# RMSNorm and matmul on one core: two stores cut at row 60, and the last two tiles stored whole

## The chip, the cores and the metric

One core of one Trainium2 chip. The time is the device time of one execution in microseconds (us); several executions are taken in turn with the kernel before on the same chip. The span in a profile is 1.8 us shorter than the time (210.6 against 212.46). A run counts as slow when it is over 1.5% above the fastest of the same kernel. Ratios use fast runs alone; medians are of all runs unless said.

## The reference

```python
x: (16, 1024, 512) float32, gamma: (512,), weight: (512, 768)
rms = np.sqrt(np.mean(x ** 2, axis=-1, keepdims=True) + eps)
x_norm = x / rms * gamma
return np.matmul(x_norm, weight).astype(np.float32)
```

The rows of x are 16384. They make 128 tiles of 128 rows. The kernel reads 33.6 MB of x and writes 50.3 MB.

## The kernel before

Tiles go in groups of 8 (16 groups). A group has one buffer of x and one of the output. It is loaded and stored in pieces given by `parts`; a piece of n tiles has n rows of DRAM in each of its 128 partitions, so a partition's run is n x 3072 B in a store (the trace has 24576 B in a store of 8 tiles, 6144 B in one of 2). Loads and stores are issued by SyncE in program order. GpSimd casts x to bf16, TensorE transposes it two pairs of tiles ahead of the matmuls, VectorE copies the transposes back, ScalarE takes the norms, and ScalarE and VectorE scale the output in turn.

```python
parts = {0: [1, 2, 1, 2, 2], 1: [4, 4], NG - 2: [4, 2, 2], NG - 1: [2, 2, 1, 1, 1, 1]}
...
def store(i):
    if i == first[i] + size[i] - 1:
        nc.sync.dma_start(out=rows(out, i), in_=held(o_tiles, first[i], size[i]))
...
for j in range(2, NP):
    load_until(2 * j + AHEAD)
    if j == NP // 2:
        marks = singles.tile([8, 2, 256], F32)
        for c, n in enumerate((5, 6)):
            nc.sync.dma_start(out=marks[:n, c, :128 + 8 * c], in_=x[:n, :128 + 8 * c])
    ...
for i in (NT - 2, NT - 1):
    for lo, hi, engine, queue in ((0, WIDE, nc.scalar, nc.scalar), (WIDE, O, nc.vector, nc.sync)):
        ...
        queue.dma_start(out=rows(out, i)[:, 0, lo:hi], in_=dst)
```

`marks` is never read. Its two loads have 5 and 6 rows of odd sizes, which makes their packets easy to find in a trace.

## Time and profile before

| | before |
|---|---|
| time, median of 3 runs (lowest to highest) | 212.46 us (212.32 to 212.94) |
| span, TensorE busy, SyncE's DMA queue busy | 210.6 us, 95%, 96.4% |
| last arithmetic ends, last store lands | 204.1 us, 209.8 us |

Two more views are needed for the comparison. First the chain of waits, by engine:

```profile
## 4 chain that ended last, share of the span: by engine, by line
PE 90%; DMA 3%; DVE 1%; ACT 1%; issue 1%; SPq 0%; DVEq 0%
```

TensorE holds nearly all of the chain. Then who waits for whom (total us, times, longest us):

```profile
POOL xb L86 <- PE tp L113: 69.4, 39, 2.0
POOL xb L86 <- DMA xt<-in_x_dram: 50.2, 16, 6.0
```

GpSimd waits more often for TensorE to free a buffer (39 times) than for a load (16 times). TensorE's only wait for a cast of GpSimd is 0.2 us: loads come in time.

The most useful records are in no summary view: the single DMA packets, with start, duration and size, and the 16 landings of a DMA on its semaphore, one from each DMA engine. A packet starts 3 to 4 ns before the one ahead of it on the same engine ends, so the packets can be strung into 16 chains, one for each DMA engine. Below, "chain" means that.

### The profile page before, as it was taken

The page shows a single profiled execution, that of the slowest core. Times are in us where ns is not written, and L with a number is a line of the kernel's source. Part 1 is how long each engine was busy: PE and PEld are TensorE (multiplying, and loading weights), DVE is VectorE, ACT ScalarE, POOL GpSimd, SP SyncE. Part 2 cuts the span into 40 slices and gives each one's busy share as a digit, 9 for nine tenths or more (in the row PEclk, how much of TensorE's full clock was granted, in tenths as well). Part 3 has the DMA queues.
Part 4 walks back from the last instruction along what each step waited for, and adds up shares of the span by engine and source line. Part 5 has one row for each costly group of instructions (what it writes and reads, how often), then busy time and mean ns, then how long its engine had stood idle before and what let it go on. Part 6 is the DMA issues. An engine that isn't in the chain of part 4 may idle for free.

```text
span 210.6 us, 3584 instructions
## 1 busy us (share of the span) xinstructions
PE 200.2 (95%) x1272; PEld 138.0 (66%) x1297; DVE 111.8 (53%) x204; ACT 158.3 (75%) x388; POOL 66.3 (31%) x71
## 2 busy tenths in 40 slices
PE   7999999999999999999999999999999999999960
PEld 2466766766776676677667666776667677766630
DVE  1555655654565456446645654565456446645630
ACT  4489777787778778877877787778778877887830
POOL 1057433423333233323242332334233323140000
PEclk9999999999999999999999999999999999999997
DMA  6999999999999999999999999999999999999892
GB/s 202 401 427 426 392 436 408 418 437 437 431 425 425 414 446 418 432 434 417 429 429 437 416 440 439 417 439 414 440 408 443 393 438 369 439 406 412 358 382 98
DMA packets 8956, 85.70 MB, mean 407 GB/s; under 512 B 1245, under 2 KB 1514, under 8 KB 5098
## 3 DMA queue, kind: packets, MB, share of 16 engines
q1 hardware_dynamic: 8374, 84.94, 96.4%
q10 hardware_dynamic: 564, 0.53, 0.7%
q8 instruction: 10, 0.16, 0.3%
q14 instruction: 8, 0.07, 0.1%
HBM read 35.14 MB, written 50.33 MB: 406 GB/s over the span
## 4 chain that ended last, share of the span: by engine, by line
PE 90%; DMA 3%; DVE 1%; ACT 1%; issue 1%; SPq 0%; DVEq 0%
PE ops L147 77%; PE tp L113 13%; DMA w_f<-in_weight_dram 3%; DVE ot L132 1%; ACT ot L130 0%; SPq L75 0%; ACT jk L90 0%; DVE w_bf L132 0%; DVE xT L120 0%; ACT rms L94 0%; DVE rstd L96 0%; DVEq L132 0%
## 5 line engine op out<-in xcount | busy, mean ns | idle before, releaser
L147 PE MATMUL ops<-w_bf,xT 128*128 128x512 bf16 (+1 forms) x999 | 192.5, 324 | 1.5 <-DVE w_bf L132 0.2
L147 PEld LDWEIGHTS <-xT 128*128 128x128 bf16 x1024 | 100.2, 98 | 56.6 <-DVE xT L120 0.9
L86 POOL CAST xb<-xt 128x1024 bf16<-128x1024 f32 (+1 forms) x65 | 65.6, 1016 | 120.2 <-PE tp L113 69.4
L120 DVE COPY xT<-tp 128x1024 bf16<-128x1024 bf16 (+1 forms) x67 | 44.5, 667 | 81.3 <-PE tp L113 81.3
L130 ACT ACTIVATE ot<-ops,rstd 128x768 f32<-128x768 f32 (+1 forms) x65 | 58.1, 894 | 37.6 <-PE ops L147 36.8
L90 ACT ACTIVATE jk<-xt 128x512 bf16<-128x512 f32 x128 | 78.8, 619 | 1.3 <-DMA xt<-in_x_dram 1.3
L113 PE MATMUL tp<-ident_f,xb 128*128 128x128 f32 x256 | 69.2, 275 | 0.4 <-DVE xb L86 0.3
L132 DVE TENSOR_SCALAR ot<-ops,rstd 128x768 f32<-128x768 f32 (+1 forms) x65 | 64.5, 992 | 2.9 <-PE ops L147 2.8
L113 PEld LDWEIGHTS tp<-ident_f,xb 128*128 128x128 f32 x256 | 36.0, 142 | 5.1 <-issue 1.2
L90 ACT ACTIVATION_READ_ACCUMULATOR jk<-xt 128x1 f32 x128 | 24.4, 191 | 0.0
L94 ACT ACTIVATE rms<-ssq,eps_sb 128x2 f32<-128x2 f32 (+1 forms) x64 | 18.9, 295 | 2.0
L96 DVE RECIPROCAL rstd<-rms 128x2 f32<-128x2 f32 (+1 forms) x64 | 9.9, 155 | 3.3 <-ACT rms L94 3.2
L202 PE MATMUL ops<-warm 128*128 128x512 bf16 x15 | 5.7, 531 | 1.2 <-DVE eps_sb L195 1.2
L130 ACT ACTIVATE w_bf<-w_f,g_sb 128x768 bf16<-128x768 f32 x2 | 1.9, 935 | 2.9 <-DMA w_f<-in_weight_dram 2.9
L202 PEld LDWEIGHTS <-warm 128*128 128x128 bf16 x15 | 1.7, 124 | 3.1 <-issue 1.4
L184 ACT ACT_TABLE_LOAD x1 | 1.3, 1283 | 1.8 <-issue 1.8
L86 DVE CAST xb<-xt 128x512 bf16<-128x512 f32 x2 | 1.2, 594 | 2.5 <-DMA xt<-in_x_dram 2.5
L132 DVE TENSOR_SCALAR w_bf<-w_f,g_sb 128x512 bf16<-128x512 f32 (+2 forms) x3 | 1.4, 485 | 1.3 <-DMA w_f<-in_weight_dram 1.3
L193 DVE MEMSET warm<- 128x256 uint32 x1 | 0.3, 272 | 0.9 <-PEq L308 0.9
L224 PE MATMUL tp<-ident_f,g_row 2*128 2x2 f32 x2 | 0.4, 264 | 0.3 <-DVE xT L120 0.3
L224 PEld LDWEIGHTS tp<-ident_f,g_row 2*128 2x128 f32 x2 | 0.3, 201 | 0.5 <-DVE xT L120 0.5
masks.py:199 POOL TENSOR_SCALAR_AFFINE_SELECT ident_f<-ident_f 128x128 f32<-128x128 f32 x1 | 0.3, 292 | 0.1
(7 smaller groups left out, 0.8 us busy)
## 6 DMA issues: line engine op xcount, KB each, us to landing
out_dram<-ot SPq DMA_DIRECT2D x12, 3072.0 KB, 14.3
xt<-in_x_dram SPq DMA_DIRECT2D x12, 2048.0 KB, 19.1
out_dram<-ot SPq DMA_DIRECT2D x7, 768.0 KB, 9.5
out_dram<-ot SPq DMA_DIRECT2D x3, 1536.0 KB, 11.8
xt<-in_x_dram SPq DMA_DIRECT2D x7, 512.0 KB, 13.8
xt<-in_x_dram SPq DMA_DIRECT2D x3, 1024.0 KB
xt<-in_x_dram SPq DMA_DIRECT2D x6, 256.0 KB, 10.3
w_f<-in_weight_dram SPq DMA_DIRECT2D x2, 768.0 KB, 7.6
```

The source lines that it names most:

```text
L86: engine.tensor_copy(out=xb_tiles[i // 2][:, i % 2:i % 2 + n, :], in_=held(x_tiles, i, n))
L90: nc.scalar.activation(out=jk, in_=held(x_tiles, i)[:, 0, :], func=AF.Square, accum_out=ssq)
L94: nc.scalar.activation(out=rms[:, :n], in_=ssq[:, :n], func=AF.Sqrt, scale=1.0 / D, bias=eps_sb)
L96: nc.vector.reciprocal(out=rstd[:, :n], in_=rms[:, :n])
L113: nc.tensor.transpose(out=tp_tiles[j][:, t, h, :], in_=words[:, lo:lo + P], identity=ident_f)
L120: nc.vector.tensor_copy(out=dst[:, t:t + n, :], in_=src[:, t:t + n, :])
L130: nc.scalar.mul(out=dst, in_=src, mul=r)
L132: nc.vector.tensor_single_scalar(out=dst, in_=src, scalar=r, op=mybir.AluOpType.mult)
L147: nc.tensor.matmul(out=acc[:, lo:hi], lhsT=xT_tiles[i // 2][:, i % 2, k // 2, :, k % 2], rhs=w_bf[:, k, lo:hi], start=(k == 0), stop=(k == ...
L184: nc.scalar.preload_act_table(AF.Sqrt)
L202: nc.tensor.matmul(out=spare[:, :WIDE], lhsT=warm[:, :P], rhs=warm, start=True, stop=True)
L224: nc.tensor.transpose(out=gp[:, c, :], in_=g_row[:, :, c], identity=ident_f[:2, :2])
```

## The change

Its intent: move some bytes from DMA engines that end late to engines that end early, and end the kernel with plain stores. The two-tile stores that end groups 5 and 10 are issued as 60 and 68 rows. The code doesn't say what that does to the engines. After each split 15 chains have 4 rows, four of them 17 more, and one has none. Below, "engines 0 to 3" are those four, "engines 4 to 14" the others of the 15, and "engine 15" the one without; the numbers are names, for no trace here shows an engine's number.

```diff
-    parts = {0: [1, 2, 1, 2, 2], 1: [4, 4], NG - 2: [4, 2, 2], NG - 1: [2, 2, 1, 1, 1, 1]}
+    SPREAD = (NG // 3, 2 * NG // 3)
+    parts = {0: [1, 2, 1, 2, 2], 1: [4, 4], NG - 2: [4, 4], NG - 1: [2, 2, 2, 1, 1]}
+    parts.update({g: [4, 2, 2] for g in SPREAD})
...
-            nc.sync.dma_start(out=rows(out, i), in_=held(o_tiles, first[i], size[i]))
+            dst, src = rows(out, i), held(o_tiles, first[i], size[i])
+            uneven = i // G in SPREAD and i % G == G - 1
+            for lo, hi in ((0, 60), (60, P)) if uneven else ((0, P),):
+                nc.sync.dma_start(out=dst[lo:hi], in_=src[lo:hi])
...
-            if j == NP // 2:
-                marks = ...            # both loads removed
...
-                dst = out_tile(i)[:, lo:hi]
-                scale(engine, dst, a[:, lo:hi], rstd_of[i])
-                queue.dma_start(out=rows(out, i)[:, 0, lo:hi], in_=dst)
+                scale(engine, out_tile(i)[:, lo:hi], a[:, lo:hi], rstd_of[i])
+            store(i)
```

More of the change, by code (lines that the diff above doesn't have):

```diff
@@ L259 @@
             load_until(2 * j + AHEAD)
-            if j == NP // 2:
-                marks = singles.tile([8, 2, 256], F32)
-                for c, n in enumerate((5, 6)):
-                    nc.sync.dma_start(out=marks[:n, c, :128 + 8 * c], in_=x[:n, :128 + 8 * c])
             if j + 3 < NP:
@@ L284 @@
         for i in (NT - 2, NT - 1):
-            for lo, hi, engine, queue in ((0, WIDE, nc.scalar, nc.scalar), (WIDE, O, nc.vector, nc.sync)):
+            for lo, hi, engine in ((0, WIDE, nc.scalar), (WIDE, O, nc.vector)):
                 a = accumulator()
```

## The prediction

> **What bounds the kernel now.** I read the page first, then the chain of waits, the SyncE queue's waits and timeline, the GpSimd timeline, and last the single records of the trace: every DMA packet with start and duration, every landing on a semaphore.
>
> ```profile
> span 210.6 us, 3584 instructions
> ...
> PE 200.2 (95%) x1272; PEld 138.0 (66%) x1297; DVE 111.8 (53%) x204; ACT 158.3 (75%) x388; POOL 66.3 (31%) x71
> ...
> DMA  6999999999999999999999999999999999999892
> GB/s 202 401 427 426 392 436 408 418 437 437 431 425 425 414 446 418 432 434 417 429 429 437 416 440 439 417 439 414 440 408 443 393 438 369 439 406 412 358 382 98
> ...
> q1 hardware_dynamic: 8374, 84.94, 96.4%
> ```
>
> Two resources are full. TensorE is busy 95% of the span, and the chain of waits is TensorE from 9 us to 203.6 us. But the 16 DMA engines are also busy 96% of the time on the one SyncE queue, so each DMA engine always has a backlog. Which of the two sets the end is decided in the last 10 us:
>
> ```profile
> core 0 of [0], span 210.6 us
> start us, us, engine line op out<-in xcount [idle before <-releaser]
> ...
> 202.06 0.33 SPq L144 DMA_DIRECT2D out_dram<-ot  x1
> 202.31 0.48 DVE L132 TENSOR_SCALAR ot<-ops,rstd 128x256 f32<-128x256 f32 x1 [0.28 <-PE ops L147]
> 202.59 0.37 ACTq L291 DMA_DIRECT2D out_dram<-ot  x1
> 203.17 0.69 ACT L130 ACTIVATE ot<-ops,rstd 128x512 f32<-128x512 f32 x1 [0.61 <-PE ops L147]
> 203.61 0.48 DVE L132 TENSOR_SCALAR ot<-ops,rstd 128x256 f32<-128x256 f32 x1 [0.82 <-PE ops L147]
> 203.89 0.35 ACTq L291 DMA_DIRECT2D out_dram<-ot  x1
> 207.61 0.81 SPq L291 DMA_DIRECT2D out_dram<-ot  x2
> ```
>
> ```profile
> engine line waited for: us in total, times, longest us
> ...
> SPq L291 <- DMA out_dram<-ot: 5.2, 1, 5.2
> ```
>
> Compute is over at 204.1 us; SyncE's last two stores go out only at 207.61 us, because the first of them waits 5.2 us for an earlier store: it has the same DMA semaphore as ScalarE's store of 202.59, whose last landing is at 207.55. They land by 209.81, and 0.84 us later the span ends. So the tail is 6.5 us of DMA after the last arithmetic.
>
> Why did that store take 5 us? Its 16 landings are not together: twelve come at 205.39 to 205.52, the others at 205.82, 206.47, 206.62 and 207.55. The store of 199.66 shows the same: twelve by 202.92, four late by 0.6, 1.2, 1.4 and 2.3 us. So a few DMA engines run behind. A packet starts 3 to 4 ns before its predecessor on the same engine ends, so the packets can be strung into 16 chains; the two tiny loads into `marks` (5 rows of 512 B, 6 rows of 544 B) name some of them. Five chains carry both a 512 and a 544 packet, a sixth only a 544. In mid-kernel every chain is gapless. The group-10 store (issued at 145.0) ends on the five marked chains at 155.74, 156.46, 157.07, 157.75 and 159.28, on the others between 155.95 and 160.3. The last of the five is slow by nature: 7.6 us per 3 MB store where the others take 7.27. By the end it is the latest of all.
>
> [...]5 and 6 rows gave 5 and 6 chains, the five contained in the six[...].[...] The trace has 8 KB fetch packets only on four of the five marked chains; their times fit ScalarE (every 54.5 us), VectorE, GpSimd, and, on the slow chain, SyncE.[...] That is an inference.
>
> **The change, part by part.**
>
> 1. *Tail.* Tiles 126 and 127 are stored whole from SyncE. There are eight stores from group 13 on, so the last needs no semaphore still in flight: the 5.2 us wait goes. Tile 126's store can go at about 202.85, tile 127's at 204.15. On a DMA engine that isn't late, the pair store for 124 and 125 (issued 202.06) ends about 205.15, then two times 0.94 us (eight 3072 B rows at 121 ns): 207.0. On today's latest engine: its 199.66 store lands at 205.05, plus four tiles at 0.95: 208.9, plus 0.84 = 209.7. With nothing else changed the span would be 210.65 - 0.9.
>
> 2. *Merged pieces* ([4,4] and [2,2,2,1,1]): the late engines have a backlog anyway, the same bytes follow in order: 0.
>
> 3. *The split stores*, the heart. In groups 5 and 10 the last two tiles (128 rows of 6144 B) go out as 60 rows on 15 engines, 4 each, and 68 rows on 4 engines, 17 each. Before, each engine moved 8 rows. Now engines 0 to 3 move 21 (+13), engines 4 to 14 move 4 (-4), engine 15 none (-8). At 0.23 us a row (234 ns less the overlap) one split is +3.0 us, -0.9 us, -1.85 us; two are +5.9, -1.85, -3.7. The slow engine, if number 4, gains 1.9 us and would finish about 206.8 to 207: good. But engines 0 to 3 never have an idle moment afterwards. They end the group-10 store at 155.74 to 157.75 now. Work left after that on one engine: loads 2 x 2.44 + 3 x 1.26 + 2 x 0.65 = 10.0; stores 3 x 7.27 + 2 x 3.67 + 3 x 1.86 + 2 x 0.95 = 36.6; together 46.6 us. Check with a late chain of today: from 160.29 to its 199.66 store's end my sum gives 43.2, the trace 43.45. The worst of four: 157.07 + 0.7 (part 4) + 5.9 + 46.6 + 0.3 for one more fetch + 0.3 for slow packets = 210.9; VectorE's chain 157.75 + 5.9 + 46.6 + 0.3 = 210.55. Landing 0.3 later, 211.2, plus 0.84: span 212.0, which is 1.4 above 210.65. So two splits overshoot: one would have about levelled the engines.
>
> 4. *Finer loads and SyncE's order.* SyncE issues in program order, and each store in the queue blocks the loads behind it:
>
> ```profile
> 72.12 0.33 SPq L144 DMA_DIRECT2D out_dram<-ot  x1
> 72.54 0.38 SPq L75 DMA_DIRECT2D xt<-in_x_dram  x1
> ```
>
> Now groups 5 and 10 have pieces stored in between, so the load of group 8 waits behind two of them: issued near 81.6 instead of 72.54, and 2.25 MB are queued ahead of it, 5.5 us. The same for group 13 (133.29, then about 142.4). Also groups 5 and 10 load only 1 MB ahead of a store: the queue runs dry for about 0.7 us on early engines (at 48.9; the store's first packet comes about 49.6). Does TensorE feel it? The GpSimd casts:
>
> ```profile
> 153.60 1.04 POOL L86 CAST xb<-xt 128x1024 bf16<-128x1024 f32 x1 [3.07 <-DMA xt<-in_x_dram]
> ...
> 183.36 1.04 POOL L86 CAST xb<-xt 128x1024 bf16<-128x1024 f32 x1 [5.51 <-DMA xt<-in_x_dram]
> ```
>
> The cast of 153.60 waits for group 13's load; its tiles are first transposed at 161.99, so 7.3 us of slack remain. With +5.5 and, on engine 3, +3.0 from its first split, that load lands near 159.9 instead of 153.5: slack about 0.9. The cast of 183.36 has 4.9 us; engines 0 to 3 bring its tiles about 2.5 to 3 us later. So no TensorE stall, narrowly; and one under 3 us would cost nothing, since the DMA ends later.
>
> 5. *Removed marks loads:* 11 packets of 28 ns: nothing.
>
> Sum: -0.9 (tail) and about +2.3 from the new latest engines: span 212.0; the time is 1.8 above the span (212.46 against 210.65): 213.9.
>
> **The rivals.**
> - *The balance works.* If engines 0 to 3 have more room than I give them (other fetches, idle stretches), the end is set by compute and the fast engines: data at 207.4 to 208.5, time 210.1 to 211.2. For it: somebody chose engines 0 to 3 with the marks in view, and four of the five marked chains are early in the trace. Against it: the sum above; their room is only 2 to 4 us, and 5.9 is put there. Weight about 0.35.
> - *The slow engine is one of the four.* It would then carry 6.2 us more on top of 208.4: landing 215, time near 217.6. For it: it is one of five marked, and four of those are loaded.[...] Weight 0.1 to 0.15.
> - *Late loads stall TensorE* more than the narrow slack: adds up to 2 us only where it passes the DMA's end. Small, inside the range.
>
> **Range and chances.** The middle case (half the weight) is 213.9, the first rival pulls the median down: 213.5, range 210.6 to 216.3. Faster by 2% needs 208.3, below even a perfectly levelled end (about 209.7): 0.01. Slower by 2% needs 216.7, which only the second rival reaches: 0.09. Same: 0.90.
>
> **What would show it.** Right, if the last stores' landings have four late engines, 3 to 5 us behind the rest, SyncE's wait of 5.2 us gone, last issue near 204.2, TensorE still ending near 203.6. GpSimd should wait some 5 to 6 us longer for DMA twice, from about 92 to 97 and from 153 to 160 us. Wrong, if the last landings lie together within 1 us (the balance works), or one engine alone is late by over 6 us (slow engine loaded), or TensorE ends after 206 (loads late).

## The result, and the profile after

| | before | changed |
|---|---|---|
| time, median (lowest to highest), 4 runs each | 212.39 us (212.13 to 212.94) | 217.96 us (217.21 to 219.75) |
| ratio of the fast runs, 95% interval | | 1.027 (1.020 to 1.034) |
| span of the profile | 210.6 us | 216.4 us |

A ratio is the mean time of one kernel's fast runs over that of the other's in the same rounds, so it is not quite the ratio of the medians. The change is slower by 2.7%; the prediction had 213.5 and a range to 216.3.

The page of the changed kernel, the lines that answer to those of before:

```profile
span 216.4 us, 3595 instructions
...
PE 200.8 (93%) x1272; PEld 137.9 (64%) x1297; DVE 111.8 (52%) x204; ACT 158.2 (73%) x388; POOL 65.5 (30%) x71
...
DMA  6999999999999999999999999999999999998871
GB/s 214 414 426 407 413 391 423 413 417 468 382 409 435 407 433 419 434 421 423 424 439 398 417 422 439 438 407 424 426 429 358 375 422 404 432 399 341 353 299 45
...
q1 hardware_dynamic: 8934, 85.46, 95.6%
...
PE 78%; DMA 12%; DVE 2%; issue 1%; POOL 1%; ACT 1%; SPq 0%; POOLq 0%
```

TensorE's work is the same (200.8 us against 200.2), in a longer span. The DMA engines are busy to nearly the same share, but right after the second split (slices 31 and 32, from 162 us on) they move 358 and 375 GB/s while still "9" busy. And DMA has 12% of the chain of waits where it had 3%.

The end, in the timeline of the last instructions:

```profile
195.90 10.91 SPq L151 DMA_DIRECT2D out_dram<-ot  x6
...
205.50 0.69 ACT L132 ACTIVATE ot<-ops,rstd 128x512 f32<-128x512 f32 x1 [0.61 <-PE ops L154]
205.93 0.48 DVE L134 TENSOR_SCALAR ot<-ops,rstd 128x256 f32<-128x256 f32 x1 [0.81 <-PE ops L154]
```

and in the waits of SyncE's queue:

```profile
SPq L324 <- DMA out_dram<-ot: 8.5, 1, 8.5
```

The 5.2 us wait between stores is gone, as intended: the last eight stores have eight different semaphores in the trace, and the last is issued at 206.48. But SyncE then waits 8.5 us for it to land. Its 16 landings tell why: twelve come from 209.47 to 209.63, four at 212.46, 213.22, 213.76 and 215.39. Four engines are late, by 3.0 to 5.9 us. In the chains these four are the ones that carried 17 packets of 6144 B in a row after each split. The steadily slow chain (7.6 us per 3 MB store against 7.27 on the others, in the kernel before, in the change and in tail only) is not among them: it carried only its 4 packets of the 60-row part.

TensorE is late too. The waits of the changed kernel:

```profile
POOL xb L88 <- DMA xt<-in_x_dram: 89.7, 21, 11.7
...
PEld tp L115 <- POOL xb L88: 3.2, 3, 1.6
```

and GpSimd's timeline:

```profile
161.86 3.99 POOL L88 CAST xb<-xt 128x1024 bf16<-128x1024 f32 x4 [11.71 <-DMA xt<-in_x_dram]
...
180.68 3.01 POOL L88 CAST xb<-xt 128x1024 bf16<-128x1024 f32 x3 [7.72 <-DMA xt<-in_x_dram]
190.49 1.04 POOL L88 CAST xb<-xt 128x1024 bf16<-128x1024 f32 x1 [6.80 <-PE tp L115]
```

The casts that begin at 161.86, 180.68 and 190.49 end 0.05 to 0.06 us before TensorE's transposes of their tiles start: three stalls, and TensorE ends 2.3 us later than before. The load of group 13 is late for the reason foreseen, SyncE's order:

```profile
132.48 9.44 SPq L151 DMA_DIRECT2D out_dram<-ot  x3
142.01 0.72 SPq L77 DMA_DIRECT2D xt<-in_x_dram  x1
144.65 0.96 SPq L151 DMA_DIRECT2D out_dram<-ot  x2
```

The load of 142.01 stands behind three stores that had to wait for their tiles, two of them pieces of group 10 that the change put there; in the kernel before the load was issued at 133.29.

So there are two candidates for the 5.6 us: the late engines at the end (theory A: bytes on engines 0 to 3), and the late loads with TensorE's stalls (theory B). A third came up during the runs (theory D): the pieces' packets get longer.

For theory B the change's own trace has an answer. The chain that ends last, at 215.07, has no gap over 20 ns from 55 us on: it always had work, so no tile that came earlier could have let it end earlier. TensorE's lateness does move the other twelve: they land 3 us after the last issue.

### The profile page after: what moved, and what is told of

Same layout as the page of the kernel before. It is cut to its first block, busy times and chain, and to the rows that moved or that the text cites.

```text
span 216.4 us, 3595 instructions
## 1 busy us (share of the span) xinstructions
PE 200.8 (93%) x1272; PEld 137.9 (64%) x1297; DVE 111.8 (52%) x204; ACT 158.2 (73%) x388; POOL 65.5 (30%) x71
## 4 chain that ended last, share of the span: by engine, by line
PE 78%; DMA 12%; DVE 2%; issue 1%; POOL 1%; ACT 1%; SPq 0%; POOLq 0%
PE ops L154 65%; DMA xt<-in_x_dram 12%; PE tp L115 12%; PE ops L209 1%; DVE ot L134 1%; POOL xb L88 1%; ACT ot L132 0%; DVE xT L122 0%; ACT jk L92 0%; DVE xb L88 0%; PE tp L231 0%; SPq L151 0%; ACT rms L96 0%; POOLq L88 0%; DVE rstd L98 0%
## 5 line engine op out<-in xcount | busy, mean ns | idle before, releaser
L88 POOL CAST xb<-xt 128x1024 bf16<-128x1024 f32 (+1 forms) x65 | 64.8, 1014 | 128.1 <-DMA xt<-in_x_dram 89.7
```

What stands on the lines that cost most here:

```text
L88: engine.tensor_copy(out=xb_tiles[i // 2][:, i % 2:i % 2 + n, :], in_=held(x_tiles, i, n))
```

## The experiments

All outputs are right. Each edit is against the changed kernel unless said. The kernel before had a median of 212.32 to 212.50 us. The medians in the table are of all runs; without the slow ones they are 213.20 (group 10 only, two slow of 7), 212.90 (group 5 only, one of 20), 219.42 (loads first, one of 4) and 219.78 (68 rows first, one of 4).

| run | splits | median us | ratio to before (95%) |
|---|---|---|---|
| tail only | none | 211.38 | 0.997 (0.995 to 0.998) |
| even halves, groups 5 and 10 | two at row 64 | 212.37 | 1.002 (1.000 to 1.004) |
| group 5 only | one | 212.91 | 1.002 (1.001 to 1.004) |
| group 10 only | one | 213.35 | 1.005 (1.002 to 1.008) |
| the change | two | 217.96 | 1.027 (1.020 to 1.034) |
| loads first | two | 219.47 | 1.032 (1.030 to 1.034) |
| 68 rows first | two | 219.81 | 1.030 (1.023 to 1.037) |
| four splits | four | 231.13 | 1.087 (1.085 to 1.090) |
| late split | one, after the last load | 215.78 | 1.016 (1.013 to 1.018) |
| late even halves | one at row 64 | 211.76 | 0.998 (0.996 to 0.999) |
| three late even halves | three at row 64 | 213.47 | 1.006 (1.004 to 1.007) |

### Is it the uneven spread, or the pieces and the order?

```diff
-            for lo, hi in ((0, 60), (60, P)) if uneven else ((0, P),):
+            for lo, hi in ((0, 64), (64, P)) if uneven else ((0, P),):
```

> The changed kernel with the same two stores cut at row 64 instead of 60: 64 rows run on all 16 DMA engines, so the number of stores, the piece sizes of groups 5 and 10 and the order in SyncE's queue stay, and only the uneven spread over DMA engines goes. Theory A (engines 0 to 3 carry 13 rows of 6144 B more per split and set the end): 211.5 to 213, the late group of four landings gone, no TensorE wait for a cast. Theory B (the finer loads and the blocked SyncE queue bring the loads late and stall TensorE): 216 to 218, as the change itself.

Measured: 212.37 us. Everything but the spread is as in the change, and 5.6 us are gone. Theory B alone is out: here, too, GpSimd waits up to 9.7 us for a load, and TensorE's wait is nearly nothing.

```profile
POOL xb L88 <- DMA xt<-in_x_dram: 75.2, 18, 9.7
...
PEld tp L115 <- POOL xb L88: 0.3, 1, 0.3
```

The opposite edit leaves the tail and takes the splits and the finer pieces away:

```diff
-    SPREAD = (NG // 3, 2 * NG // 3)
+    SPREAD = ()
```

> The change without its split groups: groups 5 and 10 in one piece as before, only the tail (tiles 126 and 127 stored whole from SyncE, pieces 4+4 and 2+2+2+1+1, marks gone). Theory A and the prediction's own tail sum: 0.9 us under the kernel before, 211.2 to 211.9, TensorE's end near 203.6, last landing on one late engine near 209. If the tail change is worth nothing: 212.3.

Measured: 211.38 us, 1.0 us under before by the medians. The tail part of the prediction holds: last landing 208.56 us, the last two stores issued without a wait. This version beats the kernel before by 0.3%, and the change by 3%. The finer pieces, the blocked loads and the even cuts cost 1.0 us together (212.37).

The attempt to take the late loads away:

```diff
-    AHEAD = 20
+    AHEAD = 24
```

> The change with loads emitted two pairs of tiles earlier (24 tiles ahead instead of 20), so that the loads of groups 8 and 13 go out right after the stores of 71.8 and 132.5 us, ahead of the store pieces that block them now, and the half loads of groups 5 and 10 no longer leave the queue short. Theory A: TensorE's waits for casts (about 2.3 us late at its end) shrink or go, but the four engines still hold the same bytes: 216 to 217.7. Theory B: the loads are in time again, 212 to 213.5.

Measured: 219.47 us, above both expectations. The edit did not do what it was to do. The loads came no earlier for TensorE, because SyncE now waits for DMA semaphores that earlier transfers still hold (7.8 us for stores and 7.7 for loads in all):

```profile
SPq L77 <- DMA out_dram<-ot: 7.8, 3, 3.3
SPq L77 <- DMA xt<-in_x_dram: 7.7, 3, 3.4
```

(This profile fell in the slow state; its times are not compared.) So it is no test of earlier loads, and it speaks neither for theory A nor against it. It does not say why it is 1.5 us slower than the change.

### How much is one split?

```diff
-            uneven = i // G in SPREAD and i % G == G - 1
+            uneven = i // G == SPREAD[1] and i % G == G - 1     # group 10 only; SPREAD[0]: group 5 only
```

> Only the store of group 10 is split 60/68, group 5 keeps its pieces but stores them whole. Theory A: one split is worth 13 rows of 0.231 us, 3.0 us, so 214.5 to 215.3; the four late engines end about 3 us earlier than with two. Theory B: no difference from the change, 217 to 218.

> Only the store of group 5 is split, group 10's is whole: the counterpart of the run with group 10 alone (213.35 us). Theory A: 212.8 to 214, since the engines are never idle between and bytes count the same in either place. Rival: only the later split matters, because an early lag is worked off before the end: 212.4, as with even halves.

Measured: 213.35 and 212.91 us (one run of the second took 1211 us and is no use). Neither theory's number for group 10 is met: by the medians one split costs 1.0 us and 0.5 us over the even halves, which is not clear of noise (ratios 1.005 and 1.002 against 1.002, the intervals overlap), and the second one 4.6 to 5.1 us more, which is. An estimate from these times: the first split fills the room that engines 0 to 3 have, and the second comes on top in full, at more than the 3.0 us of its bytes. Whether an early lag is worked off, the rival of the second run, these times don't settle.

```diff
-            uneven = i // G in SPREAD and i % G == G - 1
+            uneven = i // G in SPREAD and i % G in (G - 3, G - 1)
```

> The change with both two-tile stores of groups 5 and 10 split 60/68, so four splits instead of two, no store piece more or less otherwise. Theory A (bytes on engines 0 to 3 set the end): two more times 13 rows of 0.231 us, 6.0 us, and something for slowed packets: 223.5 to 226. Rival C (the cost comes from having a split at all, or saturates because TensorE's stalls give the queue time): under 221.

Measured: 231.13 us, 13.2 us above the change for two more splits, where the bytes explain 6.0. The sign of theory A is right, and rival C (it saturates) is out. But this is not the price of a split alone, for now TensorE does stand still, over 12 us at one time:

```profile
POOL xb L88 <- DMA xt<-in_x_dram: 108.2, 20, 21.1
...
PEld tp L115 <- POOL xb L88: 15.5, 2, 12.5
```

The arithmetic ends at 222.63 us, 16.2 us later than in the change (206.41), and 15 of the last store's 16 landings lie together at 225.67 to 225.84, one at 228.71. Here the late loads set most of the loss: what four engines hold back reaches TensorE.

```diff
-            for lo, hi in ((0, 60), (60, P)) if uneven else ((0, P),):
+            for lo, hi in ((0, 68), (68, P)) if uneven else ((0, P),):
```

> The change with the split at row 68: rows 0 to 67 on four engines first, rows 68 to 127 on fifteen after them. Same bytes per engine, other partitions. Theory A: 217 to 219, no difference from the change. If the slowed packets come from which partitions the four engines read (60 to 127 against 0 to 67), the time moves by over 1.5 us.

Measured: 219.81 us, in a range from 216.99 to 220.96 (ratio 1.030 against 1.027; the intervals overlap). By the medians it moved 1.9 us, over the 1.5 named as the sign, but with four runs, one of them slow, it decides nothing about other partitions under the four engines.

### Why is a split dearer than its bytes?

Take the split away from all loads, to a place where engines 0 to 3 have room (against the tail-only kernel):

```diff
-            uneven = i // G in SPREAD and i % G == G - 1
+            uneven = i == NT - G + 1          # the store of tiles 120 and 121
```

> The tail-only kernel (211.38 us) with one split 60/68, not in group 5 or 10 but in the store of tiles 120 and 121, after the last load, when most DMA engines have idle moments. Theory A: engines 0 to 3 have 2 to 4 us of room there and take the 3.0 us without setting the end, the slow fifth engine gives away 0.9 us: 210.5 to 211.4. The 17 rows of the four engines take 3.9 to 4.1 us, as no loads run beside them. Rival C (a split store costs by itself): 212.5 to 214.5.

Measured: 215.78 us, a clear miss: 4.4 us more than without. Bytes alone, 3.0 us, could not do that; nor is it in the range of rival C. The packets show it. In the tail-only kernel none of the 384 packets of 6144 B after 60 us takes over 330 ns (nearly all take 234). Here 87 do, and 59 of them lie between 430 and 500 ns: two times 234. The 17 rows, meant to take 3.9 us, end some 5 to 8 us after the 4 rows.

So the packets of a piece of consecutive rows may take longer than those of a whole 128-row store, whatever the bytes on each engine. Call this theory D. It has a size, the doubling measured here, but no cause that a trace shows. The test is a cut with the same bytes on every engine:

```diff
-            for lo, hi in ((0, 60), (60, P)) if uneven else ((0, P),):
+            for lo, hi in ((0, 64), (64, P)) if uneven else ((0, P),):
```

> The late-split kernel (tiles 120 and 121, 215.78 us) cut at row 64 instead of 60: every DMA engine moves 8 rows again, 4 from partitions 0 to 63 and 4 from 64 to 127. Theory A (only bytes per engine): the time of the tail-only kernel, 211.2 to 211.8, and 6144 B packets of 234 ns. Theory D[...]:[...] a good part of this store's 128 packets takes 440 to 475 ns; the time rises little, to 211.6 to 213, as the engines have idle moments after it.

> As before, with all three two-tile stores of the last group (tiles 120 to 125) cut at row 64. Theory A: 211.2 to 211.8. Theory D: each such store takes up to 3.7 us on an engine instead of 1.86 and they follow each other every 3.04 us, so the idle time no longer covers it: 213 to 216, with over 100 of the 384 packets of 6144 B near 450 ns.

(the same with `uneven = i in (NT - 7, NT - 5, NT - 3)`)

Measured: 211.76 and 213.47 us. Packets of 6144 B over 330 ns: 60 and 155 of 384, and 32 and 86 between 430 and 500 ns; without a cut 0. (The second run was to have over 100 near 450.) Every engine moves 8 rows, as in a whole store, yet many packets double, and three such cuts cost 2.1 us. Theory A alone has no place for that. In mid-kernel the same cut does little: the even halves in groups 5 and 10 have 8 of 896 such packets over 330 ns (256 of the 896 are in the cut stores), the change 17. With three even halves, twelve of the 16 engines begin the first cut store within 0.4 us (197.5 to 197.9), while in the change they come to the second split spread over 6 us (155.1 to 161.3); whether packets lengthen only when engines are in step, no run shows. The view by stretches shows the same without packets; first the tail-only kernel from 198 to 205 us (us of the stretch, busy time by engine, TensorE's clock, DMA share, GB/s), then the one with three even cuts:

```profile
198.00:205.00 7.00, 5.11 (x32) 2.90 (x30) 3.19 (x6) 3.12 (x6) 0.00 (x0) 1.00 0.91 373
```

```profile
198.00:205.00 7.00, 4.94 (x31) 2.75 (x29) 3.01 (x6) 2.95 (x6) 0.00 (x0) 1.00 0.94 288
```

The DMA engines are a little busier (0.94 against 0.91) and move a quarter less (288 GB/s against 373). So a DMA share does not tell here at what rate bytes move.

The last run asks whether smaller pieces lengthen packets more. The stores of tiles 120 to 123 are cut at rows 16, 32 and 64. That a 16-row piece would go to four times 234 ns was the estimate, not shown by an earlier run:

```diff
-            for lo, hi in ((0, 60), (60, P)) if uneven else ((0, P),):
+            for lo, hi in ((0, 16), (16, 32), (32, 64), (64, P)) if uneven else ((0, P),):    # NT - 7, NT - 5
```

> The tail-only kernel with the stores of tiles 120 to 123 (two stores) cut into rows 0-15, 16-31, 32-63 and 64-127; each piece runs on 16 DMA engines, 8 rows per engine in all as in a whole store.[...] Theory D[...]: besides the 440 to 475 ns packets there is a second group near four times 234 ns, 850 to 960 ns, up to 64 of the 256 packets of these two stores (fewer, as late engines are out of step). If the doubling in the even halves had another cause (the writes to HBM, or the number of pieces): durations stay at 440 to 475 ns or fall back to 234.

Measured in one look: 212.43 us (before beside it 212.81). The first piece's packets on the engines that were in step took 439 to 912 ns, with one of 1531, so three to four times 234 for most, which is what the expectation had under theory D. But 23 packets of this kernel passed 640 ns, and so did 21 with three even halves and 9 with one (up to 1056 ns), where a doubling of 234 gives 468. And the second piece, rows 16-31, which is as small, went mostly at 234 ns. A factor that follows from the size of the piece gives neither. Why the second piece escapes is open.

### What the runs add up to

Over the whole kernel, each DMA engine spent this much on packets beyond the usual duration of their size (mean of 16 engines, from 20 us on): 2.7 us in the kernel before, 2.5 tail only, 5.1 in the change, 8.4 with four splits. Bytes put on four engines (theory A) and longer packets (shown; why they are longer is not) make the loss together. Longer packets in the pieces, as theory D has it, don't account for all of it. The even halves of groups 5 and 10 have 3.0 us by the same count; of the 2.1 us that the change has more, only 0.3 lie in packets of 6144 B, the rest mostly in whole loads and stores beside the splits (0.8 in loads of 8192 B a row, up to 1942 ns a packet instead of 309). And in the kernel before, where nothing is cut, 12 packets of whole stores from 160 to 180 us took over 1.4 times their usual 912 ns, up to 1811. The late loads stall TensorE, but in the change the last chain never ran dry, so the stall doesn't set the end.

## Why the prediction was wrong

- **Tail, -0.9 us: right.** The tail-only kernel is 1.0 us faster by the medians. Of the signs that were named, the four late engines came (3.0 to 5.9 us behind) and the 5.2 us wait went; but the last issue was at 206.48, not near 204.2, as TensorE was late.
- **Which engines: right.** Chains with 4 and 17 rows, one chain without any, the slow engine outside the four: all in the trace of the change. That the slow engine would be outside was the estimate before the result. The rival that put the slow engine under the load has nearly the right time (217.6) for a wrong reason: luck.
- **"At 0.23 us a row ... one split is +3.0 us": the step that failed.** It takes a row's price from whole stores, and the price of the load behind from loads that have no split beside them. In the change the 17 rows took 3.92, 3.92, 4.75 and 5.09 us in the first split and 4.66, 4.70, 4.79 and 5.10 in the second, against 3.93, and the load behind took 2.9 to 3.5 us instead of 2.44.
- **The sum for the worst engine, 210.9, was 4.2 us low.** For the chain that was last, step by step:

| | predicted us | measured us |
|---|---|---|
| begins its 4 rows of the second split (155.2 + 0.7 + 3.0) | 158.9 | 161.3 |
| ends its 17 rows | 163.8 | 166.9 |
| ends the half load behind it | 166.2 | 170.4 |
| last data written | 210.9 | 215.1 |

  The first 2.4 us have three sources: the four engines came to the first split at 95.0 to 95.7, about 1.0 later than my 0.7 us for the dry queue allowed (why is open); the first split's slow rows gave 0.8 on this chain (4.75 us, up to 1.2 on another); the rest is longer packets between the splits. Then 0.7 and 1.1 more at the second. The sum for VectorE's chain, 210.55, also left out the 0.7 us and the slow packets that the other one has. The 44 us after that fit within 0.1.
- **"One would have about levelled the engines": wrong.** By the medians one split cost 0.5 to 1.0 us over even halves (not clear of noise), and 1.5 to 2.0 over none.
- **"No TensorE stall, narrowly; and one under 3 us would cost nothing":** it stalled, 2.3 us in all, because the landings came later than summed. That it cost nothing is what the last chain without a gap says; no run separates it.
- **Range and chance.** 0.09 for slower was too low: every miss found on the last chain (1.0, 0.8, 0.6, 0.7 and 1.1 us) went the same way, towards later, and the range had no case for that.

## What to carry to other kernels

Moving bytes between DMA engines by choosing odd row counts cost more here than the bytes say (one late split 4.4 us where the bytes give 3.0): packets of the pieces, and of transfers beside them, got longer (87 of 384 packets of 6144 B over 330 ns in the late split, none without it; in the change loads of 8192 B up to 1942 ns instead of 309), for a reason that no run shows. Prefer whole 128-row transfers, and price a change in the spread from a run that has such a piece, not from whole transfers. On the last chain here, which had no gap over 20 ns from 55 us on, the lag stayed to the end: the four engines landed 3.0 to 5.9 us behind, from splits whose 68 rows had landed some 50 and 115 us before; check how much room such an engine has before giving it more. And a lag that holds back loads can grow into stalls of the compute, as with four splits (one wait of TensorE of 12.5 us).
